# A gated MLP's first products with tokens on partitions, turned back through VectorE and DRAM

## The chip, the cores and the metric

The kernel runs on one core of one Trainium2 chip. The metric is the device time of one execution in microseconds. Five engines work side by side, each through its own list of instructions in order: TensorE (PE, with its weight loads PEld), VectorE (DVE), ScalarE (ACT), GpSimd (POOL) and SyncE (SP), which here only issues DMAs. An instruction whose input is late holds up everything behind it on its engine.

## The reference

One decoder layer on 256 tokens of width 2048, all in float32. The change is in its second half, the gated MLP:

```
h = rmsnorm(x, norm_ffn_w)                        # 256 x 2048
gate, up = split(h @ w_up, 2)                     # w_up 2048 x 11264, so 2 x (256 x 5632)
gate = causal_dwconv(gate, conv_ffn_w) + bias     # along the tokens, width 3, per feature
x = x + (gelu(gate) * up) @ w_down                # w_down 5632 x 2048
```

## The kernel before

Every float32 matrix is split into a rounded part and its remainder, `hi` and `lo` (type float32r), and a product is three: hi x hi, lo x hi, hi x lo.

**Weights.** `weights()` hands out the next tile of a fixed list `srcs`: 256 rows by 512 columns, 512 KB. `begin()` (L105 to L120) issues its load on SP into `raw` (four buffers, L110), ACT rounds it into `whi` (three buffers, L112), and DVE subtracts to get `wlo` (three buffers, L119). It does so two tiles ahead. The order in which each engine runs its instructions is not the order of the code: a scheduler of the framework arranges the rows of each engine at build time by its own idea of the times, and the order is then fixed.

**Two forms of product.** `gemm_a` (L138) keeps tokens on the partitions of the result: the activations are the stationary side (128 x 128) and the weights move, 512 columns at a time. For each of 16 slices of 128 rows and each of the two token halves it issues three matmuls of 512 columns (L149, L150, L151), 96 for a product of 2048 by 512. It first runs what stands in the list `later` after its first weight tile. `gemm_b` (L157) keeps features on partitions: the weights are stationary, and the activations' `hi` and `lo`, side by side in `fhl` (256 tokens each), move. For each slice and each of four groups of 128 features it issues one matmul of 512 columns (whi with hi and lo, L173) and one of 256 (wlo with hi, L174), 128 for a product. Its result has two halves for each group; `merged` (L178) copies one half out on ACT (L182) and adds the other on DVE (L183).

**The stage around the change** (L808 to L837) walks over the 5632 features in 11 blocks of 512. For a block: a `gemm_b` for gate; its merging; a multiplication by `rb2`, the norm's factor of each token laid along the free dimension (L814); the convolution along the tokens, 12 DVE instructions (L818, L822), which needs features on partitions; gelu on ACT (L824); a multiplication by `rb2` on POOL (L825); a `gemm_b` for up; its merging; the product with the gelu (L827); and the split of the result into `hhi` and `hlo` (L834, L835). These are the stationary side of the down stage (L854 to L864), 22 x 4 weight tiles of 12 matmuls each. Ahead of the stage stands the output projection, by `gemm_a` (L780 to L801).

**Block turns and DRAM elsewhere.** In the token mixer, four times, the kernel also writes a small tile to DRAM in pieces of 128 bytes (`cdd`, L554: 128 partitions of eight pieces), reads it back in another arrangement (`lb`, L557), and turns 32 x 32 blocks on DVE (L587, L621).

Of the kernel before, what the change touches and what calls it, by code (L numbers as in the profile page):

```python
# [33 lines left out]
def kernel(  # L34
# [32 lines left out]
    def nm(s):  # L67
        cnt[0] += 1
        return f"{s}_{cnt[0]}"

    def pg(shape=(P, 512)):
        return psg.tile(list(shape), F32, tag="g", name=nm("psg"))
# [26 lines left out]
    def weights():  # L99

        begin(taken[0] + AHEAD + 1)
        taken[0] += 1
        return made[taken[0] - 1]
# [28 lines left out]
    def pm():  # L132
        return psm.tile([P, 2, 512], F32, tag="m", name=nm("psm"))


    later = []

    def gemm_a(lh, ll, nk, steps=None, ps=None):  # L138

        ps = pm() if ps is None else ps  # L140
        for c in range(nk // 2) if steps is None else steps:
            if c == 1:
                while later:
                    later.pop(0)()
            hi, lo = weights()
            for kk in range(2):
                k = 2 * c + kk
                for t in range(2):
                    mm(ps[:, t, :], lh(k, t), hi[:, kk, :], start=(k == 0), stop=False)  # L149
                    mm(ps[:, t, :], ll(k, t), hi[:, kk, :], start=False, stop=False)  # L150
                    mm(ps[:, t, :], lh(k, t), lo[:, kk, :], start=False, stop=(k == nk - 1))  # L151
                side()
        return ps

    banks = [0]

    def gemm_b(rhl, nk):  # L157

        banks[0] ^= 1
        if banks[0]:
            pair = [pm(), pm()]
            ps = [pair[f // 2][:, f % 2].rearrange("p (a s) -> p a s", a=2) for f in range(4)]
        else:
            ps = [pg([P, 2, S]) for f in range(4)]
        for c in range(nk // 2):
            hi, lo = weights()
            for f in range(4):
                fs = slice(f * P, (f + 1) * P)  # L170
                for kk in range(2):
                    k = 2 * c + kk
                    mm(ps[f], hi[:, kk, fs], rhl(k), start=(k == 0), stop=False, skip_group_check=True)  # L173
                    mm(ps[f][:, 1, :], lo[:, kk, fs], rhl(k)[:, 0, :], start=False, stop=(k == nk - 1),  # L174
                       skip_group_check=True)
        return ps

    def merged(ps, dst):  # L178

        for f in range(4):  # L180
            low_half = fp.tile([P, S], F32, tag="lh", bufs=3, name=nm("lh"))
            nc.scalar.copy(low_half, ps[f][:, 1, :])  # L182
            nc.vector.tensor_tensor(dst[:, f, :], ps[f][:, 0, :], low_half, op=ALU.add)  # L183
        return dst

    def turned(src):

# [11 lines left out]
    ones = cpool.tile([P, P], F32, name="ones")  # L199
    nc.gpsimd.memset(ones, 1.0)  # L200
    ident = cpool.tile([P, P], F32, name="ident")
# [27 lines left out]
    for k2 in range(KD // 2):  # L229
        pt = pg([P, 2, S])  # L230
        for kk in range(2):
            k = 2 * k2 + kk
# [3 lines left out]
        for kk in range(2):  # L236
            k = 2 * k2 + kk
            nc.scalar.activation(xhi[:, k, :], pt[:, kk, :], AF.Copy, scale=nmw[:, k : k + 1])  # L238
            nc.vector.scalar_tensor_tensor(xlo[:, k, :], pt[:, kk, :], nmw[:, k : k + 1], xhi[:, k, :].bitcast(F32),
                                           op0=ALU.mult, op1=ALU.subtract)  # L240
# [47 lines left out]
    gwb = mp.tile([P, P], F32, name="gwb")  # L288
    nc.scalar.dma_start(gwb, gdn_norm_w[0].partition_broadcast(P))

    def rstd_rows(ssq, dst):


        ms = cpool.tile([P, 2], F32, name=nm("ms"))
        nc.vector.tensor_scalar(ms, ssq, 1.0 / D, EPS, op0=ALU.mult, op1=ALU.add)
        rs = cpool.tile([P, 2], F32, name=nm("rs"))
        nc.gpsimd.tensor_tensor(rs, ms, epsx, op=ALU.pow)
        if dst is None:
            return rs
        pr = pg()  # L300
        for t in range(2):
            dg = cpool.tile([P, P], F32, tag="diag", bufs=2, name=nm("diag"))
            nc.vector.tensor_scalar(dg, ident, rs[:, t : t + 1], None, op0=ALU.mult)
            mm(pr[:, t * P : (t + 1) * P], ones, dg, start=True, stop=True)
        nc.vector.tensor_copy(dst, pr[:, :S])
        return rs

    ssq4 = cpool.tile([P, 2, 4], F32, tag="ssq4", name="ssq4a")
# [3 lines left out]
            nc.scalar.activation(junk, x0[c][:, t, :], AF.Square, accum_out=ssq4[:, t, c : c + 1])  # L312
    ssq = cpool.tile([P, 2], F32, name="ssq")
    nc.vector.tensor_reduce(ssq, ssq4, axis=mybir.AxisListType.X, op=ALU.add)
    rs1 = rstd_rows(ssq, None)
    rsh = cpool.tile([P, 2], F32, name="rsh")
    nc.vector.tensor_scalar(rsh, rs1, 0.5, None, op0=ALU.mult)
    rsq = cpool.tile([P, 2], F32, name="rsq")
# [27 lines left out]
    for cq in range(4):  # L346
        pr = slice(32 * cq, 32 * cq + 32)
# [18 lines left out]
    for c in range(2):  # L366
        hi, lo = weights()
        for kk in range(8):
            k = 8 * c + kk
# [57 lines left out]
    for g, win in enumerate(WINDOWS):  # L427
# [3 lines left out]
        for cs in (slice(0, P + PAD), slice(P + PAD, NB)):  # L431
            b = bd[:, cs]
# [255 lines left out]
    for g in range(4):  # L688
        kq = mp.tile([P, 4, 2, S], F32, tag="kq", bufs=1, name=nm("kq"))
        vT = mp.tile([P, 4, S], F32, tag="vT", bufs=1, name=nm("vT"))  # L690
        for kind, dst in ((1, kq[:, :, 0, :]), (0, kq[:, :, 1, :]), (2, vT)):
# [3 lines left out]
            ps = ps_k0 if kind == 1 and g == 0 else gemm_a(xh, xl, KD)  # L695
            e = evict(ps)
# [5 lines left out]
        ps = gemm_a(xh, xl, KD)  # L702
        e = evict(ps)
# [97 lines left out]
                                               op0=ALU.mult, op1=ALU.subtract)  # L801
    ssq2 = cpool.tile([P, 2], F32, name="ssq2")
    nc.vector.tensor_reduce(ssq2, ssq4, axis=mybir.AxisListType.X, op=ALU.add)
    rb2 = cpool.tile([P, S], F32, tag="rb", name="rb2")
    rstd_rows(ssq2, rb2)


    hhi = []  # L808
    hlo = []
    rb2b = rb2.unsqueeze(1).to_broadcast([P, 4, S])  # L810
    for c in range(DFF // 512):
        ps = gemm_b(lambda k: fhl[:, k], KD)
        gs = fp.tile([P, 4, S], F32, tag="gs", bufs=2, name=nm("gs"))
        nc.vector.tensor_tensor(gs, merged(ps, gs), rb2b, op=ALU.mult)  # L814
        y = fp.tile([P, 4, S], F32, tag="y", name=nm("y"))
        for f in range(4):
            r = 4 * c + f
            nc.vector.tensor_scalar(y[:, f, :], gs[:, f, :], cfw[:, 2 * KF + r : 2 * KF + r + 1],  # L818
                                    vec[:, V_CB + r : V_CB + r + 1], op0=ALU.mult, op1=ALU.add)
            for j in (1, 0):  # L820
                s = 2 - j
                nc.vector.scalar_tensor_tensor(y[:, f, s:], gs[:, f, : S - s], cfw[:, j * KF + r : j * KF + r + 1],  # L822
                                               y[:, f, s:], op0=ALU.mult, op1=ALU.add)
        nc.scalar.activation(y, y, AF.Gelu)  # L824
        nc.gpsimd.tensor_tensor(y, y, rb2b, op=ALU.mult)  # L825
        ps = gemm_b(lambda k: fhl[:, k], KD)
        nc.vector.tensor_tensor(gs, merged(ps, gs), y, op=ALU.mult)  # L827
        if c < 4:
            hh = mtile(c, [P, 4, S], F32R, f"hhi{c}")
            hl = mtile(4 + c, [P, 4, S], F32R, f"hlo{c}")  # L830
        else:
            hh = fp.tile([P, 4, S], F32R, name=f"hhi{c}")
            hl = fp.tile([P, 4, S], F32R, name=f"hlo{c}")
        nc.scalar.copy(hh, gs)  # L834
        nc.vector.tensor_tensor(hl, gs, hh.bitcast(F32), op=ALU.subtract)  # L835
        hhi.append(hh)
        hlo.append(hl)  # L837

    nfin = big.tile([P, D], F32, tag="xhl", name="nfin")
    nc.scalar.dma_start(nfin, norm_final_w.partition_broadcast(P))  # L840
# [75 lines left out]
```

## Time and profile before

| | |
|---|---|
| median of 3 runs | 1590.08 us (1589.59 to 1591.71) |
| span of the profiled execution | 1591.1 us |
| first matmul of gate and up to first of the down stage | 848.3 to 1341 us |
| down stage | 1341 to 1580 us |
| HBM read, written | 287.07 MB, 3.15 MB |

The profiled execution is one of its own; its span lies 1.0 us above the median. In a group's row stand line, engine, operation, output and inputs with shapes, count, then busy time in total, the mean of one in ns, and the engine's idle time just before them. Matmuls overlap in the pipeline, so the mean of one (390 ns) is longer than their spacing; the spacing is read from a stretch of time and the count in it.

### The profile page before, as it was taken

The page shows a single profiled execution, that of the slowest core. Times are in us where ns is not written, and L with a number is a line of the kernel's source. Part 1 is how long each engine was busy: PE and PEld are TensorE (multiplying, and loading weights), DVE is VectorE, ACT ScalarE, POOL GpSimd, SP SyncE. Part 2 cuts the span into 40 slices and gives each one's busy share as a digit, 9 for nine tenths or more (in the row PEclk, how much of TensorE's full clock was granted, in tenths as well). Part 3 has the DMA queues.
Part 4 walks back from the last instruction along what each step waited for, and adds up shares of the span by engine and source line. Part 5 has one row for each costly group of instructions (what it writes and reads, how often), then busy time and mean ns, then how long its engine had stood idle before and what let it go on. Part 6 is the DMA issues. An engine that isn't in the chain of part 4 may idle for free.

```text
span 1591.1 us, 21437 instructions
## 1 busy us (share of the span) xinstructions
PE 1568.4 (99%) x8116; PEld 1318.2 (83%) x8116; DVE 1065.8 (67%) x1624; ACT 750.2 (47%) x969; POOL 116.7 (7%) x132
## 2 busy tenths in 40 slices
PE   8999999999999999999999999999999999999997
PEld 6888888888888888787888888888888888888886
DVE  5778757786678757786565777666666677444445
ACT  5545435444545445544454544444444444333334
POOL 3020100110020100102000000000000000000000
PEclk9999999999999999999999999999999999999998
DMA  7656656566556656565656666666666666666563
GB/s 248 181 156 193 192 147 173 166 194 173 159 151 194 191 153 174 164 190 173 203 185 182 187 189 191 188 186 187 186 196 186 187 191 208 200 193 198 190 194 133
DMA packets 160605, 291.62 MB, mean 183 GB/s; under 512 B 18022, under 2 KB 21110, under 8 KB 160374
## 3 DMA queue, kind: packets, MB, share of 16 engines
q1 hardware_dynamic: 157792, 285.77, 61.2%
q10 hardware_dynamic: 2710, 4.48, 0.8%
q8 instruction: 63, 1.03, 0.3%
q14 instruction: 40, 0.33, 0.1%
HBM read 287.07 MB, written 3.15 MB: 182 GB/s over the span
## 4 chain that ended last, share of the span: by engine, by line
PE 89%; DMA 3%; DVE 3%; issue 2%; POOL 2%; SPq 1%; ACT 0%; DVEq 0%; POOLq 0%
PE psm L151 13%; PE psm L150 12%; PE psm L149 12%; PE psm L173 10%; PE psg L173 10%; PE psg L174 5%; PE psm L174 5%; PE psg L850 3%; PE psg L851 3%; PE psg L852 3%; PE psm L851 2%; PE psm L850 2%; PE psm L852 2%; DVE wlo L119 1%; PE psg L519 1%
## 5 line engine op out<-in xcount | busy, mean ns | idle before, releaser
L119 DVE TENSOR_TENSOR wlo<-raw,whi 128x1024 fp32r<-128x1024 f32 x528 | 657.2, 1246 | 412.9 <-ACT whi L112 406.6
L112 ACT CAST whi<-raw 128x1024 fp32r<-128x1024 f32 x530 | 557.8, 1053 | 752.7 <-PE psm L150 342.9
L151 PE MATMUL psm<-wlo,xhl 128*128 128x512 f32 x896 | 353.3, 394 | 2.9 <-DVE wlo L119 2.9
L149 PE MATMUL psm<-whi,xhl 128*128 128x512 f32 x896 | 352.5, 393 | 1.7 <-ACT xhl L238 1.7
L150 PE MATMUL psm<-whi,xhl 128*128 128x512 f32 x896 | 352.1, 393 | 0.0
L173 PE MATMUL psm<-fhl,whi 128*128 128x512 f32 x704 | 245.9, 396 | 0.0
L173 PE MATMUL psg<-fhl,whi 128*128 128x512 f32 x704 | 237.8, 394 | 0.0
L151 PEld LDWEIGHTS psm<-wlo,xhl 128*128 128x128 f32 x896 | 168.7, 188 | 38.7 <-DVE wlo L119 4.5
L149 PEld LDWEIGHTS psm<-whi,xhl 128*128 128x128 f32 x896 | 168.9, 188 | 35.7 <-ACT xhl L238 2.1
L150 PEld LDWEIGHTS psm<-whi,xhl 128*128 128x128 f32 x896 | 168.9, 188 | 34.9
L174 PE MATMUL psm<-fhl,wlo 128*128 128x256 f32 x704 | 194.2, 279 | 0.0
L174 PE MATMUL psg<-fhl,wlo 128*128 128x256 f32 x704 | 178.6, 279 | 0.0
L173 PEld LDWEIGHTS psm<-fhl,whi 128*128 128x128 f32 x704 | 131.3, 188 | 30.4
L173 PEld LDWEIGHTS psg<-fhl,whi 128*128 128x128 f32 x704 | 129.2, 188 | 24.1
L174 PEld LDWEIGHTS psg<-fhl,wlo 128*128 128x128 f32 x704 | 132.4, 188 | 6.9
L174 PEld LDWEIGHTS psm<-fhl,wlo 128*128 128x128 f32 x704 | 132.5, 188 | 1.1
L850 PE MATMUL psg<-whi,hhi 128*128 128x512 f32 x176 | 68.6, 390 | 0.0
L851 PE MATMUL psg<-whi,hlo 128*128 128x512 f32 x176 | 68.5, 389 | 0.0
L850 PE MATMUL psm<-whi,hhi 128*128 128x512 f32 x176 | 68.5, 389 | 0.0
L851 PE MATMUL psm<-whi,hlo 128*128 128x512 f32 x176 | 68.5, 389 | 0.0
L852 PE MATMUL psm<-wlo,hhi 128*128 128x512 f32 x176 | 68.5, 389 | 0.0
L852 PE MATMUL psg<-wlo,hhi 128*128 128x512 f32 x176 | 61.6, 389 | 0.0
(233 smaller groups left out, 1515.7 us busy)
## 6 DMA issues: line engine op xcount, KB each, us to landing
raw<-in_w_in_dram SPq DMA_DIRECT2D x226, 512.0 KB, 3.8
raw<-in_w_up_dram SPq DMA_DIRECT2D x176, 512.0 KB, 3.8
raw<-in_w_down_dram SPq DMA_DIRECT2D x88, 512.0 KB, 3.7
raw<-in_w_out_dram SPq DMA_DIRECT2D x32, 512.0 KB, 3.7
raw<-in_pool_w_dram SPq DMA_DIRECT2D x8, 512.0 KB, 3.9
x<-in_x_dram SPq DMA_DIRECT2D x4, 512.0 KB, 7.7
lb<-cdd SPq DMA_DIRECT2D x16, 128.0 KB, 2.9
xt<-in_x_dram ACTq DMA_DIRECT2D x4, 512.0 KB, 7.9
```

The lines of the kernel that those rows point to most:

```text
L112: nc.scalar.copy(hi, raw)
L119: nc.vector.tensor_tensor(lo, raw, hi.bitcast(F32), op=ALU.subtract)
L149: mm(ps[:, t, :], lh(k, t), hi[:, kk, :], start=(k == 0), stop=False)
L150: mm(ps[:, t, :], ll(k, t), hi[:, kk, :], start=False, stop=False)
L151: mm(ps[:, t, :], lh(k, t), lo[:, kk, :], start=False, stop=(k == nk - 1))
L173: mm(ps[f], hi[:, kk, fs], rhl(k), start=(k == 0), stop=False, skip_group_check=True)
L174: mm(ps[f][:, 1, :], lo[:, kk, fs], rhl(k)[:, 0, :], start=False, stop=(k == nk - 1), skip_group_check=True)
L519: mm(pg0, kq[:, h, 0, 0:P], kq[:, h, :, :], start=True, stop=True)
L850: mm(acc[c][t], lh(k, t), hi[:, kk, :], start=(k == 0), stop=False)
L851: mm(acc[c][t], ll(k, t), hi[:, kk, :], start=False, stop=False)
L852: mm(acc[c][t], lh(k, t), lo[:, kk, :], start=False, stop=(k == KF - 1))
```

## The change

Gate and up are computed by `gemm_a`, tokens on partitions, 96 matmuls of 512 columns each; `gemm_b`, `merged` and `rb2` go. `features` evicts the result on ACT with the token's norm factor as scale (L788 of the new program), two instructions of 512 columns. `flip` then moves features to partitions: DVE turns every 32 x 32 block of the 128 x 1024 tile in one instruction (L158), four DMAs (L162), one for each 32 partitions, write the blocks to a DRAM tile of 512 features by 256 tokens in pieces of 32 tokens (128 bytes, 1024 pieces a DMA), and one DMA (L164) reads that tile back with features on partitions, in pieces of 1 KB. All five are issued on SP. The convolution and gelu, and the product and split, become functions that are put on `later`, and so are written into the code after the first weight tile of the next product. `y` and the gate's result have two buffers each. The other functions are as they were.

```
+    def flip(pool, src, tag, bufs):
+        b = pool.tile([P, 2, 512], F32, tag="tn", name=nm("tn"))
+        nc.vector.transpose(b.rearrange("p t f -> p (t f)"), src.rearrange("p t f -> p (t f)"))
+        d = dpool.tile([512, S], F32, tag="flip", name=nm("flip"))
+        dv = d.rearrange("(f i) (t a j) -> a i t f j", i=32, t=2, j=32)
+        for a in range(4):
+            nc.sync.dma_start(dv[a], b[32 * a : 32 * a + 32].rearrange("p t (f j) -> p t f j", j=32))
+        o = pool.tile([P, 4, S], F32, tag=tag, bufs=bufs, name=nm(tag))
+        nc.sync.dma_start(o, d.rearrange("(f p) s -> p f s", p=P))
+        return o
...
+    rs2 = rstd(ssq2)
...
+    def features(ps):
+        e = fp.tile([P, 2, 512], F32, tag="ev", name=nm("fev"))
+        for t in range(2):
+            nc.scalar.activation(e[:, t, :], ps[:, t, :], AF.Copy, scale=rs2[:, t : t + 1])
+        return flip(fp, e, "gs", 2)
...
-    rb2b = rb2.unsqueeze(1).to_broadcast([P, 4, S])
-    for c in range(DFF // 512):
-        ps = gemm_b(lambda k: fhl[:, k], KD)
-        gs = fp.tile([P, 4, S], F32, tag="gs", bufs=2, name=nm("gs"))
-        nc.vector.tensor_tensor(gs, merged(ps, gs), rb2b, op=ALU.mult)
-        y = fp.tile([P, 4, S], F32, tag="y", name=nm("y"))
+    def gated_linear(c, gs, y):
         for f in range(4):
...
         nc.scalar.activation(y, y, AF.Gelu)
-        nc.gpsimd.tensor_tensor(y, y, rb2b, op=ALU.mult)
-        ps = gemm_b(lambda k: fhl[:, k], KD)
-        nc.vector.tensor_tensor(gs, merged(ps, gs), y, op=ALU.mult)
+
+    def product(us, y, hh, hl):
+        nc.vector.tensor_tensor(y, us, y, op=ALU.mult)
+        nc.scalar.copy(hh, y)
+        nc.vector.tensor_tensor(hl, y, hh.bitcast(F32), op=ALU.subtract)
+
+    for c in range(DFF // 512):
+        gs = features(gemm_a(fh, fl, KD))
+        y = fp.tile([P, 4, S], F32, tag="y", bufs=2, name=nm("y"))
+        later.append(lambda c=c, gs=gs, y=y: gated_linear(c, gs, y))
+        us = features(gemm_a(fh, fl, KD))
...
+        later.append(lambda us=us, y=y, hh=hh, hl=hl: product(us, y, hh, hl))
...
+    while later:
+        later.pop(0)()
```

The scheduler's order in the stage, at the two places of which the prediction speaks. Weight tiles of `w_up` are numbered from 0, eight to a product, so the gate product of the second block has tiles 16 to 23; names carry running numbers.

SP, after that gate product. Before, its rows in the whole stage are weight loads alone, one like the other. Now (raw_7916 is tile 30, raw_7934 tile 31, raw_7952 tile 32, raw_7970 tile 33):

```order
L110 DMA raw_7898<-in_w_up_dram 128x2x512
L110 DMA raw_7916<-in_w_up_dram 128x2x512
L162 DMA flip_7822<-tn_7820 64x16x32 x4
L110 DMA raw_7934<-in_w_up_dram 128x2x512
L110 DMA raw_7952<-in_w_up_dram 128x2x512
L164 DMA gs_7827<-flip_7822 128x4x256
L110 DMA raw_7970<-in_w_up_dram 128x2x512
```

The four writes stand behind the load of tile 30; the loads of tiles 31 and 32 come between the writes and the read, and four more loads after tile 33's follow before the next product's writes.

DVE, from a gate product's end to the end of the next product. Before (the gate product ends ahead of the first L183 row; `psm` is its result, `lh` the copied half):

```order
L183 TENSOR_TENSOR gs_8334<-psm_8156,lh_8335 128x256
L119 TENSOR_TENSOR wlo_8371<-raw_8367,whi_8369 128x1024
L183 TENSOR_TENSOR gs_8334<-psm_8156,lh_8338 128x256
L183 TENSOR_TENSOR gs_8334<-psm_8157,lh_8341 128x256
L119 TENSOR_TENSOR wlo_8393<-raw_8389,whi_8391 128x1024
L183 TENSOR_TENSOR gs_8334<-psm_8157,lh_8344 128x256
L814 TENSOR_TENSOR gs_8334<-gs_8334,rb_7335 128x1024
L119 TENSOR_TENSOR wlo_8415<-raw_8411,whi_8413 128x1024
L818 TENSOR_SCALAR y_8348<-gs_8334,cfw,vec 128x256 x4
L822 SCALAR_TENSOR_TENSOR y_8348<-gs_8334,cfw,y_8348 128x255 x3
```

Now (wlo_7835 is tile 26, the third after the gate product's end; wlo_7920 is tile 30, wlo_7938 tile 31, wlo_7956 tile 32; `fev` is the evicted result, `tn` the turned one, `gs` what the read brings):

```order
L119 TENSOR_TENSOR wlo_7835<-raw_7831,whi_7833 128x1024
L158 STREAM_TRANSPOSE tn_7820<-fev_7817 128x1024
L119 TENSOR_TENSOR wlo_7866<-raw_7862,whi_7864 128x1024
L119 TENSOR_TENSOR wlo_7884<-raw_7880,whi_7882 128x1024
L119 TENSOR_TENSOR wlo_7902<-raw_7898,whi_7900 128x1024
L119 TENSOR_TENSOR wlo_7920<-raw_7916,whi_7918 128x1024
L797 TENSOR_SCALAR y_7829<-gs_7827,cfw,vec 128x256 x4
L801 SCALAR_TENSOR_TENSOR y_7829<-gs_7827,cfw,y_7829 128x255 x4
L119 TENSOR_TENSOR wlo_7938<-raw_7934,whi_7936 128x1024
L801 SCALAR_TENSOR_TENSOR y_7829<-gs_7827,cfw,y_7829 128x254 x4
L119 TENSOR_TENSOR wlo_7956<-raw_7952,whi_7954 128x1024
```

Before, the convolution stood two weight tiles behind the end of its product and read what DVE itself had just written; now it stands four tiles behind the turn and reads what a DMA brings. After an up product, the product with the gelu (L806) has the convolution's place, with one wlo behind it, then the split.

More of the change, by code (lines that the diff above doesn't have):

```diff
@@ L153, in gemm_a @@
         return ps
[L155 to L184, printed above, removed]
+    def flip(pool, src, tag, bufs):
[8 more added lines that the diff above has]
+        return o
     def turned(src):
@@ L289, with rstd @@
     nc.scalar.dma_start(gwb, gdn_norm_w[0].partition_broadcast(P))
-    def rstd_rows(ssq, dst):
+    def rstd(ssq):
         ms = cpool.tile([P, 2], F32, name=nm("ms"))
@@ L297, in rstd_rows @@
         nc.gpsimd.tensor_tensor(rs, ms, epsx, op=ALU.pow)
[L298 to L305, printed above, removed]
         return rs
@@ L314 @@
     nc.vector.tensor_reduce(ssq, ssq4, axis=mybir.AxisListType.X, op=ALU.add)
-    rs1 = rstd_rows(ssq, None)
+    rs1 = rstd(ssq)
     rsh = cpool.tile([P, 2], F32, name="rsh")
@@ L803, with fh, fl @@
     nc.vector.tensor_reduce(ssq2, ssq4, axis=mybir.AxisListType.X, op=ALU.add)
-    rb2 = cpool.tile([P, S], F32, tag="rb", name="rb2")
-    rstd_rows(ssq2, rb2)
+    rs2 = rstd(ssq2)
+    def fh(k, t):
+        return fhi[:, k, t * P : (t + 1) * P]
+    def fl(k, t):
+        return flo[:, k, t * P : (t + 1) * P]
+    def features(ps):
[3 more added lines that the diff above has]
+        return flip(fp, e, "gs", 2)
     hhi = []
     hlo = []
-    rb2b = rb2.unsqueeze(1).to_broadcast([P, 4, S])
-    for c in range(DFF // 512):
-        ps = gemm_b(lambda k: fhl[:, k], KD)
-        gs = fp.tile([P, 4, S], F32, tag="gs", bufs=2, name=nm("gs"))
-        nc.vector.tensor_tensor(gs, merged(ps, gs), rb2b, op=ALU.mult)
-        y = fp.tile([P, 4, S], F32, tag="y", name=nm("y"))
+    def gated_linear(c, gs, y):
         for f in range(4):
@@ L833 @@
             hl = fp.tile([P, 4, S], F32R, name=f"hlo{c}")
-        nc.scalar.copy(hh, gs)
-        nc.vector.tensor_tensor(hl, gs, hh.bitcast(F32), op=ALU.subtract)
+        later.append(lambda us=us, y=y, hh=hh, hl=hl: product(us, y, hh, hl))
         hhi.append(hh)
         hlo.append(hl)
+    while later:
+        later.pop(0)()
     nfin = big.tile([P, D], F32, tag="xhl", name="nfin")
```

## The prediction

> **What bounds the kernel now.** I read the engine totals, then the chain that ended last, then the groups of instructions, then a table by stretches of time.
>
> ```profile
> PE 1568.4 (99%) x8116; PEld 1318.2 (83%) x8116; DVE 1065.8 (67%) x1624; ACT 750.2 (47%) x969; POOL 116.7 (7%) x132
> PE 89%; DMA 3%; DVE 3%; issue 2%; POOL 2%; SPq 1%; ACT 0%; DVEq 0%; POOLq 0%
> L173 PE MATMUL psm<-fhl,whi 128*128 128x512 f32 x704 | 245.9, 396 | 0.0
> L174 PE MATMUL psm<-fhl,wlo 128*128 128x256 f32 x704 | 194.2, 279 | 0.0
> ```
> ```profile
> 1360.00:1560.00 200.00, 200.00 (x884) 165.59 (x883) 89.50 (x74) 78.07 (x74) 0.00 (x0) 1.00 0.62 194
> 848.30:1341.00 492.70, 492.70 (x2828) 430.21 (x2827) 336.84 (x434) 238.72 (x293) 28.05 (x12) 1.00 0.64 188
> ```
>
> TensorE is busy 99% of the span and makes up 89% of the chain; the matmuls of gate and up waited 0.0 us. The second fence holds, for each stretch, its length and the busy time (and count) of PE, PEld, DVE, ACT and POOL, then the granted clock, the DMA share and GB/s. In 848.30 to 1341.00, the stretch of gate and up, PE never stops, so the time there is the number of matmuls times their spacing. Nothing that DVE, ACT or POOL does there costs anything, unless it makes PE wait.
>
> **PE, the gain.** Of 2828 matmuls, 2816 are the 1408 pairs of a 512 wide and a 256 wide one; the other 12 are small and take about 1.2 us (eight 128 wide ones ran 1.05 us, row in the fence below). So a product of 64 pairs takes (492.7 - 1.2) / 22 = 22.34 us. The new form has 96 matmuls, all 512 wide, the form of the down stage, where the first row gives 200.00 / 884 = 0.2262 us each: 21.72 us. The columns streamed are equal (64 x 768 = 96 x 512), so the 0.62 us are what the narrow matmuls cost beyond their width. 22 x 0.62 = **13.7 us** gained if PE still never waits.
>
> **DVE, ACT, POOL, off the path.**
>
> ```profile
> 757.02 1.05 PE L648 MATMUL psg<-w,ga 128*128 128x128 f32 x8
> L183 DVE TENSOR_TENSOR gs<-psm,lh 128x256 f32<-128x256 f32 x44 | 17.4, 417 | 0.0
> L814 DVE TENSOR_TENSOR gs<-gs,rb 128x1024 f32<-128x1024 f32 x11 | 13.5, 1225 | 0.4
> L182 ACT COPY lh<-psg 128x256 f32<-128x256 f32 x44 | 16.3, 370 | 4.3 <-PE psg L174 2.0
> L450 ACT ACTIVATE ev<-psm,rs 128x512 f32<-128x512 f32 x32 | 20.2, 681 | 1.6 <-PE psm L151 1.6
> L587 DVE STREAM_TRANSPOSE tcm<-tct x4: 445/446/448, 179.4 to 718.8; 128x256 f32<-128x256 f32 x4
> L621 DVE STREAM_TRANSPOSE TT<-T 32x128 f32<-32x128 f32 x16 | 4.8, 302 | 0.5
> ```
>
> DVE loses 88 additions of 0.417 and 11 scalings of 1.225 us (50 us) and gains 22 turns of 1024 columns. No row has that size: 256 columns took 446 ns and 128 took 302, 1.125 ns a column, so about 1.3 us (four times 446, 1.8, at most): 29 to 39 us. ACT loses 88 copies of 0.37 and gains 44 evictions of 0.68 us: even. POOL loses the scaling of L825. All that is covered by PE. On SP come 110 more DMAs: per product four writes and one read.
>
> **The new chain, and where it can reach PE.** Count from t = 0, the end of a gate product, in the order shown on DVE (tile 24 is then the next on PE). The tempo of the other engines:
>
> ```profile
> 762.21 1.05 ACT L112 CAST whi<-raw 128x1024 fp32r<-128x1024 f32 x1 [1.67 <-PE psm L150]
> 762.24 0.39 PE L149 MATMUL psm<-whi,mhi 128*128 128x512 f32 x1
> 763.30 1.23 DVE L119 TENSOR_TENSOR wlo<-raw,whi 128x1024 fp32r<-128x1024 f32 x1 [1.50 <-ACT whi L112]
> ```
> ```profile
> 661.01 0.40 SPq L554 DMA_DIRECT2D cdd<-cd  x1
> 665.68 1.90 SPq L557 DMA_DIRECT2D lb<-cdd  x4
> raw<-in_w_up_dram SPq DMA_DIRECT2D x176, 512.0 KB, 3.8
> ```
>
> A cast starts as PE ends a tile (three buffers), the subtraction follows, done 2.3 us after the tile's end. So: cast to 1.05, eviction 2 x 0.68 to 2.4, turn 1.3, hand-overs 0.1: the block is turned at **3.9**. Then the writes. The one in the trace of this kind is cdd: 1024 pieces of 128 bytes, as one of the four here. Its packets by stretch (1.00 us of the burst, its fastest quarter, and a stretch of another such write with weights between, 0.50 us; then a weight load, 2 KB packets, 1.25 us, and by stretches its fastest 0.5 us):
>
> ```profile
> DMA packets 1043, 0.22 MB, mean 224 GB/s; under 512 B 997, under 2 KB 997, under 8 KB 1042
> DMA packets 358, 0.05 MB, mean 213 GB/s; under 512 B 357, under 2 KB 357, under 8 KB 357
> q1 hardware_dynamic: 357, 0.04, 115.4%
> DMA packets 473, 0.14 MB, mean 276 GB/s; under 512 B 432, under 2 KB 432, under 8 KB 473
> q1 hardware_dynamic: 473, 0.14, 124.7%
> DMA packets 207, 0.41 MB, mean 329 GB/s; under 512 B 6, under 2 KB 6, under 8 KB 207
> q1 hardware_dynamic: 207, 0.41, 91.6%
> ...
> 904.50:905.00 0.50, 0.50 (x4) 0.43 (x4) 0.50 (x1) 0.00 (x0) 0.00 (x0) 1.00 1.00 389
> ```
>
> That is 864 to 1428 pieces a microsecond; I take 1000, the mean of a whole burst. 4096 pieces need 4.1 us (2.9 to 4.7). The loads show some 1.75 us from issue to the bulk of the packets and 0.6 from the last packet to landing (3.8 less 1.4 to 1.5 of data; estimates). Written: 3.9 + 1.75 + 4.1 = 9.75; SP issues the read at 10.4. But two weight loads stand ahead of it in SP's order, behind the writes: 0.524 MB at 389 GB/s, 1.35 us each, to 12.45. The read, 512 KB in pieces of 1 KB, 1.6 us (by the two rates, 389 and 329 GB/s, 1.35 to 1.6; smaller packets, so the slower), and landing: **14.6**, with bounds 13.4 and 15.2 from the piece rate.
>
> Who waits: the convolution on DVE for that read; behind it stands the subtraction of tile 31, and PE for that. PE starts tile 31 at 7 x 2.715 = 19.0 and reads its wlo 0.45 later; tile 32's at 22.2. DVE needs, after the read lands,
>
> ```profile
> L818 DVE TENSOR_SCALAR y<-gs,cfw,vec 128x256 f32<-128x256 f32 x44 | 15.2, 408 | 0.0
> L822 DVE SCALAR_TENSOR_TENSOR y<-gs,cfw,y 128x255 f32<-128x255 f32 x44 | 19.2, 479 | 0.0
> L119 DVE TENSOR_TENSOR wlo<-raw,whi 128x1024 fp32r<-128x1024 f32 x528 | 657.2, 1246 | 412.9 <-ACT whi L112 406.6
> ```
>
> 4 x 0.408 + 4 x 0.479 = 3.55, wlo 1.24, 4 x 0.478 = 1.9, wlo 1.24: 7.9 us, to 22.2. So a gate block may land as late as **14.3**; each microsecond later is one of PE, 11 times. An up block only has a 1.23 us product and one wlo before 19.5: limit 17.0. The six weight loads queued behind the read on SP are due at 10.5 and need 3.8 us before their cast at 19.0: 4.7 us of cover. The last blocks of the stage have the whole down stage; its accumulator that waits for the last eviction (2.5) comes fourth in turn (8.1).
>
> The sum: 1591.1 (the profiled span) - 13.7 + 11 x 0.3 (14.6 against 14.3) = 1580.7; the median of the runs is 1.0 below that span, so **1580**. With 13.4 it is 1576, with 15.2 (0.9 late) 1586: the forecast's own range, with 2 us for the rate of PE, is 1574 to 1588.
>
> The Trainium skill ("DMA: Bandwidth & Descriptors", "Rules for kernel authors") warns against a plain DMA with a rearranged pattern for a transposition, 19 times slower than the hardware's. By it a block would take 19 x 1.35 = 26 us, an estimate, longer than a product, and the sum would be some 1912 us. The rows disagree: 128-byte pieces cost 2.9 to 4.7 us a block, two to four times a weight load, since the turn of 32 x 32 blocks on DVE leaves them whole.
>
> **Rivals.** (a) *The block lands late.* The four writes take from 32 partitions each, cdd from 128, and four follow one another; no row shows either. At two thirds of my rate (665 a us) they take 6.2 us, the block lands at 16.7, 2.4 late: 1576 + 26, **1602**; at half, 18.7: gates 4.4, ups 1.7 late, 11 x 6.1 = 67, about 1643. It turns slower from 15.8 on (11 x 1.5 = 13.7 + 3). For it: one hand-over of 1 us that I missed suffices. Against: the trace's writes at full pace. (b) *The DMA engines fill.* By time of packets: 0.64 x 22.4 = 14.3 us a product now; 16 x 0.25 x 1.154 / 357 = 13 ns a piece (21 by the slower stretch), 4096 / 16 of them 3.3 to 5.4; the read at 88 ns, 2.8: 20.4 to 22.5 of 21.7. For it, that sum; against, that packet times stretch when nobody waits: 0.41 MB in 1.25 us is 329 GB/s, and 5.2 MB in 21.7 only 241. If it holds, loads queue and a product takes some 24 us: 1591 + 22 x 1.7 = 1628. (c) *The crossing paces the stage.* At 200 pieces a microsecond, a fifth of the row, the writes take 20.5 us; with 8 x 1.35 of weights and 1.6 of read the queue needs 33 us a product: 1591 + 22 x 10.5 = 1822. For it: scattered 1 KB steps in DRAM; against: cdd scatters as widely. The Trainium skill's rule above would act here as this does. (d) *No gain*: the wide matmuls run at 0.233 here, or the lateness eats the gain: 1590. Against the first: the same form at 0.2262 in the down stage, with as much DMA.
>
> **How the numbers follow.** Forecast 0.55; (a) 0.22; (b) 0.06; (c) 0.02; (d) 0.15, mostly lateness between 15.3 and 15.8. This kernel's measurement tells no less than 0.2%, 3 us, from no change, so faster 0.55, same 0.15, slower 0.30. The time is that of the forecast. The range goes from 1574 to 1620 (landing 17.6: 3.3 and 0.6 late, 1576 + 43), leaving 0.03 below and 0.12 above, for half the rate, (c) and part of (b).
>
> **What would show it.** Matmul spacing 0.226 in the stage, and a stage of 478 to 482 us instead of 492.7. The first convolution (L797) waits for a DMA, and the wlo behind it is what PE waits for, in the last tile before or the first of the next gate product, 0 to 1 us each. The turn near 1.3 us, and 128-byte packets near 1000 a us. If PE waits elsewhere, for casts or raw tiles, then (b); if it waits over 1.5 us at each gate, then (a). I am wrong if the stage is longer than 492 us, or if PE is gapless with pairs no cheaper.

## The result, and the profile after

The changed kernel takes 1581.36 us (1580.43 to 1587.84), the kernel before, beside it, 1589.80 (1589.55 to 1591.71): a ratio of **0.9949, with a 95% interval of 0.9935 to 0.9964**. The prediction was 1580, in a range of 1574 to 1620. The profiled execution of the changed kernel took 1581.35 us, its span is 1579.6.

The engine totals and the shares of the chain that ended last, of the changed kernel:

```profile
PE 1556.7 (99%) x7408; PEld 1284.3 (81%) x7408; DVE 1040.2 (66%) x1544; ACT 745.8 (47%) x925; POOL 89.4 (6%) x121
PE 86%; DMA 4%; DVE 4%; issue 3%; SPq 1%; POOL 1%; ACT 0%; DVEq 0%; POOLq 0%
```

PE is busy 11.7 us less than the 1568.4 of before and still makes up 86% of the chain. Next, stretches of the stage (length, busy time and count of PE, PEld, DVE, ACT and POOL, granted clock, DMA share, GB/s). First the kernel before:

```profile
860.00:1330.00 470.00, 470.00 (x2695) 410.24 (x2694) 320.69 (x411) 225.10 (x274) 24.86 (x10) 1.00 0.65 189
```

Then the changed kernel, whose last row is the down stage:

```profile
860.00:1330.00 470.00, 468.12 (x2058) 385.34 (x2057) 300.00 (x343) 224.81 (x235) 0.00 (x0) 1.00 0.79 237
1360.00:1560.00 200.00, 200.00 (x884) 165.62 (x883) 90.40 (x74) 77.47 (x74) 0.00 (x0) 1.00 0.57 190
```

PE now has short gaps in the stage. Summed over the starts of successive matmuls, by how much each start came later than 0.2262 us after the last (differences under 0.01 us left out), they are 3.8 us; (470 - 3.8) / 2058 is 0.2265 us, so between the gaps the wide matmuls run at the down stage's pace. The DMA share rose from 0.65 to 0.79.

The waits of the stage (us in total, times, longest) show what makes the gaps:

```profile
DVE y L806 <- DMA gs<-flip: 30.9, 10, 3.6
DVE y L797 <- DMA gs<-flip: 23.1, 11, 3.7
PEld psm L151 <- DVE wlo L119: 4.8, 7, 1.4
PE psm L151 <- DVE wlo L119: 1.4, 2, 0.9
```

DVE waits at each of the 11 convolutions (L797) and at 10 of the products (L806) for the block read back; of that, PE sees a few microseconds, through a late `wlo`. One gate block in order of time (start, length, engine, line; the gate product ends at 999.38, the prediction's t = 0):

```profile
999.38 1.05 ACT L112 CAST whi<-raw 128x1024 fp32r<-128x1024 f32 x1 [1.62 <-PE psm L150]
1000.34 1.26 ACT L788 ACTIVATE fev<-psm,rs 128x512 f32<-128x512 f32 x2
1001.63 1.25 DVE L158 STREAM_TRANSPOSE tn<-fev 128x1024 f32<-128x1024 f32 x1
1002.90 4.42 SPq L162 DMA_DIRECT2D flip<-tn  x4
1007.42 1.15 SPq L110 DMA_DIRECT2D raw<-in_w_up_dram  x2
1009.87 0.37 SPq L164 DMA_DIRECT2D gs<-flip  x1
1015.07 1.38 DVE L797 TENSOR_SCALAR y<-gs,cfw,vec 128x256 f32<-128x256 f32 x4 [2.50 <-DMA gs<-flip]
1017.95 1.21 DVE L119 TENSOR_TENSOR wlo<-raw,whi 128x1024 fp32r<-128x1024 f32 x1
1020.66 3.48 DVE L119 TENSOR_TENSOR wlo<-raw,whi 128x1024 fp32r<-128x1024 f32 x3
```

The block is turned at 3.5, its read issued at 10.5, and it has landed at 15.7. It is one of 11: the convolutions of the gate blocks start 13.9 to 16.9 us after their product's end, 15.3 on average. The latest, where the gate product ends at 1086.9, and PE at its first gap:

```profile
1103.79 1.38 DVE L797 TENSOR_SCALAR y<-gs,cfw,vec 128x256 f32<-128x256 f32 x4 [3.73 <-DMA gs<-flip]
1107.94 0.50 PE L151 MATMUL psm<-wlo,fhl 128*128 128x512 f32 x1 [0.94 <-DVE wlo L119]
```

The turn and the issues of the writes (ns, shortest, median and longest):

```profile
L162 SPq DMA_DIRECT2D flip<-tn x88: 581/667/3589, 872.1 to 1340.0; - x88
L158 DVE STREAM_TRANSPOSE tn<-fev x22: 1230/1245/1247, 870.8 to 1332.9; 128x1024 f32<-128x1024 f32 x22
```

And the DMA issues (KB each, median us from issue to landing):

```profile
raw<-in_w_up_dram SPq DMA_DIRECT2D x176, 512.0 KB, 4.5
flip<-tn SPq DMA_DIRECT2D x88, 128.0 KB, 4.7
gs<-flip SPq DMA_DIRECT2D x22, 512.0 KB, 4.7
```

**A measure for the experiments.** The work ahead of the stage is the same code in most of these kernels, yet its end moves by a few microseconds between profiled executions (the stage's first matmul stood at 848.3 us before, at 845.9 in the changed kernel, at 851.2 in another run). Where a trace is spoken of below, I therefore count from that first matmul to the end of the span: before 1591.1 - 848.3 = 742.8 us, now 1579.6 - 845.9 = 733.7, 9.1 us less.

### The profile page after: what moved, and what is told of

Its sections match the earlier page's. It is cut to its first block, busy times and chain, and to the rows that moved or that the text cites. A ratio compares the mean times of both kernels' runs of the same rounds, so it can differ in the third digit from the quotient of the medians.

```text
span 1579.6 us, 20017 instructions
## 1 busy us (share of the span) xinstructions
PE 1556.7 (99%) x7408; PEld 1284.3 (81%) x7408; DVE 1040.2 (66%) x1544; ACT 745.8 (47%) x925; POOL 89.4 (6%) x121
## 4 chain that ended last, share of the span: by engine, by line
PE 86%; DMA 4%; DVE 4%; issue 3%; SPq 1%; POOL 1%; ACT 0%; DVEq 0%; POOLq 0%
PE psm L151 22%; PE psm L150 21%; PE psm L149 21%; PE psg L840 3%; PE psm L839 3%; PE psg L839 2%; PE psm L838 2%; PE psg L838 2%; PE psm L840 2%; DVE wlo L119 2%; DMA gs<-flip 1%; SPq L162 1%; PE psg L491 1%; DMA flip<-tn 1%; PE psg L175 1%
## 5 line engine op out<-in xcount | busy, mean ns | idle before, releaser
L119 DVE TENSOR_TENSOR wlo<-raw,whi 128x1024 fp32r<-128x1024 f32 x528 | 648.5, 1233 | 376.1 <-ACT whi L112 368.6
L151 PE MATMUL psm<-wlo,fhl 128*128 128x512 f32 x704 | 273.7, 390 | 1.9 <-DVE wlo L119 1.4
L150 PE MATMUL psm<-whi,fhl 128*128 128x512 f32 x704 | 274.0, 389 | 0.0
L149 PE MATMUL psm<-whi,fhl 128*128 128x512 f32 x704 | 273.9, 389 | 0.0
L151 PEld LDWEIGHTS psm<-wlo,fhl 128*128 128x128 f32 x704 | 132.1, 188 | 32.0 <-DVE wlo L119 4.8
L150 PEld LDWEIGHTS psm<-whi,fhl 128*128 128x128 f32 x704 | 132.2, 188 | 27.6
L149 PEld LDWEIGHTS psm<-whi,fhl 128*128 128x128 f32 x704 | 132.2, 188 | 27.1
L439 DVE SCALAR_TENSOR_TENSOR cy<-psg,cqw,cy 128x255 f32<-128x255 f32 (+1 forms) x144 | 60.5, 473 | 0.4 <-ACT cy L436 0.4
L151 PE MATMUL psm<-wlo,mhi 128*128 128x512 f32 x128 | 50.0, 391 | 0.3 <-DVE wlo L119 0.3
```

What stands on the lines that cost most here:

```text
L119: nc.vector.tensor_tensor(lo, raw, hi.bitcast(F32), op=ALU.subtract)
L439: nc.vector.scalar_tensor_tensor(y[:, f, s:], gs[:, : S - s], w(j), y[:, f, s:], op0=ALU.mult, op1=ALU.add)
```

## Experiments

The theory: the pace of the wide matmuls gives 13.7 us, and the wait of the convolution for the block read back takes some 4 of them. The rivals for the missing part are that the pace is worth less, that the added traffic costs, or that one of the queues does. All diffs are against the changed kernel. The times of before, beside the runs, were 1591.9 to 1592.05 us.

### 1. Without the way through DRAM

The turn writes straight into the tile that the convolution reads; the features then lie in the wrong places.

```
-        b = pool.tile([P, 2, 512], F32, tag="tn", name=nm("tn"))
-        nc.vector.transpose(b.rearrange("p t f -> p (t f)"), src.rearrange("p t f -> p (t f)"))
...
-        for a in range(4):
-            nc.sync.dma_start(dv[a], b[32 * a : 32 * a + 32].rearrange("p t (f j) -> p t f j", j=32))
...
-        nc.sync.dma_start(o, d.rearrange("(f p) s -> p f s", p=P))
+        nc.vector.transpose(o.rearrange("p f s -> p (f s)"), src.rearrange("p t f -> p (t f)"))
```

> Leaves out the way through DRAM: the 32x32 block turn on VectorE writes straight into the tile that the convolution and the product read, so features stand in the wrong places, but every other instruction is there. Theory (the pace of the wide matmuls is worth 13.7 us and the PE gaps of 3.8 us in the changed kernel come from blocks that land late): no gaps are left, the stage runs at 0.2262 us a matmul, 1577.5 us (1576.5 to 1578.5), 4 us under the changed kernel. Rival (the crossing is hidden, and what is missing of the gain is the pace itself): 1581, as the changed kernel.

Measured: 1578.80 us, ratio 0.9915 [0.9903, 0.9927]; from the stage's start to the end 729.6 us, 13.2 less than before. The same stretch of the stage:

```profile
860.00:1330.00 470.00, 470.00 (x2075) 389.20 (x2074) 306.19 (x347) 229.20 (x239) 0.00 (x0) 1.00 0.66 193
```

No gap is left on PE. So the pace is worth 13.2 us of the 13.7 predicted, and the way through DRAM costs 733.7 - 729.6 = 4.1, against 3.8 us of gaps. This says that the way through DRAM costs it, not yet how.

### 2. The convolution held two weight tiles later

The way through DRAM and its traffic stay whole. The convolution is put into the order of DVE behind the subtraction of tile 32, and the product with the gelu comes two tiles later as well. (`subs` lists the subtractions; `issue_after` places what it encloses behind one of them.)

```
     def gated_linear(c, gs, y):
+        with tc.issue_after(subs[taken[0] - 1].ins):
+            convolved(c, gs, y)
...
     def product(us, y, hh, hl):
-        nc.vector.tensor_tensor(y, us, y, op=ALU.mult)
+        with tc.issue_after(subs[taken[0] - 1].ins):
+            nc.vector.tensor_tensor(y, us, y, op=ALU.mult)
...
+        if c:
+            later.append(prod)
+        us = features(gemm_a(fh, fl, KD))
         later.append(lambda c=c, gs=gs, y=y: gated_linear(c, gs, y))
-        us = features(gemm_a(fh, fl, KD))
...
-        later.append(lambda us=us, y=y, hh=hh, hl=hl: product(us, y, hh, hl))
+        prod = lambda us=us, y=y, hh=hh, hl=hl: product(us, y, hh, hl)
```

> The change whole, and on VectorE the convolution is queued two weight tiles later (behind the subtraction of tile 32 of the prediction's count, done near 18.6 us after the gate product's end, while the block lands near 15.7), the product with the gelu two tiles later too. Theory (only the order on VectorE makes PE wait for a block): no gaps of PE in the stage, as without the way through DRAM, so 0.9915 of the kernel before, 1576.5 to 1579. Rival (the blocks' DMAs slow the weights themselves, or a later convolution makes the next turn late and the wait moves there): gaps remain, 1581 or more.

Measured: 1579.18 us, ratio 0.9919 [0.9905, 0.9933]; 730.1 us from the stage's start. The stage, and DVE around one convolution (its line is L805 here, the subtraction's L120):

```profile
860.00:1330.00 470.00, 470.00 (x2076) 389.16 (x2075) 305.11 (x347) 228.45 (x239) 0.00 (x0) 1.00 0.83 240
```
```profile
1017.11 1.22 DVE L120 TENSOR_TENSOR wlo<-raw,whi 128x1024 fp32r<-128x1024 f32 x1 [1.50 <-ACT whi L113]
1018.25 1.38 DVE L805 TENSOR_SCALAR y<-gs,cfw,vec 128x256 f32<-128x256 f32 x4
```

The convolution starts without a wait, and PE has no gap, at a DMA share of 0.83, higher than the changed kernel's 0.79. So the traffic itself costs nothing; all of the 4 us comes from the place in DVE's order of what reads the block: it stood ahead of a `wlo`, and waited there.

To be sure of so small a difference, both ran again side by side on one chip:

> The whole change with the convolution held behind the subtraction of tile 32, again, on the same chip as the changed kernel as it is. Theory (its gain is the 3.8 us of PE gaps that the wait for the read back costs): ratio 0.992, about 3 us below the changed kernel beside it. Rival (the difference between the two was one of chips): the two agree within 1 us.

> The changed kernel as it is, beside the one with the convolution held later. Theory: ratio 0.9945 to 0.995, PE gaps of 3 to 5 us at the gates. Rival: 0.992, no different from the held one.

Measured: held later 1580.16 us, 0.9923 [0.9911, 0.9935], 729.7 us from the stage's start; as it is 1584.58 us, 0.9954 [0.9942, 0.9967], 733.8, with 3.5 us of PE gaps. The difference is 4.4 us. Not all of these gaps stand at the gates: 1.2 us of them lie behind three up blocks, where it is the product with the gelu (L806) that waits. For one of them, whose up product ends at 1022.3:

```profile
1040.41 1.22 DVE L806 TENSOR_TENSOR y<-gs,y 128x1024 f32<-128x1024 f32 x1 [4.45 <-DMA gs<-flip]
1042.83 0.50 PE L151 MATMUL psm<-wlo,fhl 128*128 128x512 f32 x1 [0.38 <-DVE wlo L119]
```

So holding the product later is part of the remedy too. Holding both later beats both kernels.

### 3. The read back on another queue

```
-        nc.sync.dma_start(o, d.rearrange("(f p) s -> p f s", p=P))
+        nc.gpsimd.dma_start(o, d.rearrange("(f p) s -> p f s", p=P))
```

> Only the read back of the block is issued on GpSimd's queue in place of SP's, so it no longer stands behind two weight loads. Theory (lateness decides, and about 2.7 us of it is those two loads): the block lands 2 to 2.7 us earlier, near 13.3 us after the product's end where the limit is some 15, the gaps before the first tiles of a gate product vanish: 1577.5 to 1578.5. Rival (the two loads are not what delays it, or GpSimd's queue is slower to start by as much): 1581 or more.

Measured: 1603.29 us, ratio 1.0075 [1.0062, 1.0089]. The prediction's chain has the read behind two weight loads in SP's order; I expected it to land earlier if it had a queue of its own. It landed later:

```profile
gs<-flip POOLq DMA_DIRECT2D x22, 512.0 KB, 5.9
```
```profile
DVE y L797 <- DMA gs<-flip: 38.5, 10, 4.3
PEld psm L151 <- DVE wlo L119: 25.7, 28, 1.9
```
```profile
1025.92 1.38 DVE L797 TENSOR_SCALAR y<-gs,cfw,vec 128x256 f32<-128x256 f32 x4 [4.06 <-DMA gs<-flip]
```

From issue to landing took 5.9 us instead of 4.7. The start makes the difference, as the rival has it: on GpSimd's queue the read's first packet comes 2.8 to 4.1 us after the issue, on SP's 1.6 to 2.4, while the packets then take about as long (2.4 us on average, 2.6 on SP's queue) among about as many bytes of weights (0.40 MB, 0.36). In the block of the last row the gate product ends at 1008.67 and the convolution starts 17.2 us later; over the 11 gate blocks it is 17.1 us on average, in the changed kernel 15.3. The convolutions waited 38.5 us instead of 23.1, and PE's gaps came to 23 us instead of 3.8. So 1.8 us more lateness multiplied the price of the crossing by six, as the prediction's rival (a) has it ("It turns slower from 15.8 on").

The two loads ahead of the read, which I took for a cost that could be avoided, did not hold up its issue. In the changed kernel SP issues them while the writes are under way, and what it then waits for, here over the whole stage, is the landing of the writes:

```profile
SPq L164 <- DMA flip<-tn: 24.8, 32, 1.3
```

A queue of the read's own has that wait as well.

### 4. Writes and read on that queue

The same edit for the four writes too.

> The four writes and the read are issued on GpSimd's queue. Theory (SP's queue held by the writes is what delays, 4.4 us of issue a block): SP's weight loads flow as before, the blocks land by 14, 1577.5 to 1579. Rival (making 1024 descriptors a DMA takes GpSimd longer than SP): the writes take several us more, the block lands after 16, gaps of 1 to 5 us at each gate, 1590 to 1630.

Measured: 1592.48 us (1585.76 to 1600.18 in ten executions), ratio 1.0004 [0.9988, 1.0020], no different from before. Writes and reads both take 5.6 us to land:

```profile
flip<-tn POOLq DMA_DIRECT2D x88, 128.0 KB, 5.6
gs<-flip POOLq DMA_DIRECT2D x22, 512.0 KB, 5.6
```

The rival held: the gate blocks come 16.6 to 21.5 us after their product's end, not by 14. PE's gaps in the profiled execution are 14.7 us (1.5 of them matmuls at half the granted clock, behind a gap of 3.3 us), and 744.8 us pass from the stage's start, 2.0 more than before: 13.2 gained and 14.7 lost are 1.5. The queue is not all that changed: five `wlo` now stand between a turn and its convolution on DVE and six between a turn and its product, where the changed kernel has four. That order moves the limit to some 18 us (a gate block at 17.6 left no gap, one at 18.3 cost 0.3 us) and so spares PE much of the wait; this run does not price the queue alone. The spread of these executions is wider than any other kernel's here; what makes it so was not settled.

### 5. Each block written twice

Four more writes for each block, to a DRAM tile that nothing reads.

```
+        d2 = dpool.tile([512, S], F32, tag="flip2", name=nm("flip2"))
+        dv2 = d2.rearrange("(f i) (t a j) -> a i t f j", i=32, t=2, j=32)
+        for dd in (dv2, dv):
+            for a in range(4):
+                nc.sync.dma_start(dd[a], b[32 * a : 32 * a + 32].rearrange("p t (f j) -> p t f j", j=32))
```

> Each block is written to DRAM twice, first to a tile that nobody reads: four more writes of 1024 pieces stand ahead of the read. Theory (each microsecond of a block beyond its limit is one of PE): the block lands some 4.5 us later, near 20 us; 4.5 to 5 us at each gate and 2 to 3 at each up block, 11 times: 70 to 90 us on 1579, so 1650 to 1670, more if the clock falls in gaps that long. Rival (the crossing has room, the gaps of the changed kernel are chance): under 1600.

Measured: 1610.72 us (two executions, 1606.83 and 1614.60), ratio 1.0117 [1.0089, 1.0145]. The size was missed, by some 50 us: I had taken the order on DVE as it was, and the scheduler put the convolution one `wlo` later and the product two, so that the convolution's wait for the block stayed as it was. Instead weight loads came late:

```profile
DVE wlo L119 <- ACT whi L112: 163.7, 82, 6.8
ACT whi L112 <- DMA raw<-in_w_up_dram: 122.3, 55, 7.0
...
DVE y L800 <- DMA gs<-flip: 23.0, 10, 3.4
```
```profile
860.00:1330.00 470.00, 454.75 (x1971) 368.66 (x1970) 284.45 (x324) 214.68 (x225) 0.00 (x0) 1.00 0.90 250
```
```profile
1009.60 7.04 SPq L165 DMA_DIRECT2D flip<-tn  x8
1016.74 1.68 SPq L110 DMA_DIRECT2D raw<-in_w_up_dram  x3
```

The casts (`whi`) waited 122.3 us for weights. The third fence is SP's own time: eight writes occupy it for 7.0 us, and the loads behind them are issued only then. The DMA share is 0.90 on average and GB/s hardly rose (250 after 237). Whether SP's issue or the fill of the DMA engines makes the loads late, this run can't tell apart; it shows how near rival (b) stood: with twice the pieces its sign came, casts that wait for weights, and the kernel took 15.8 us more than before (1604.7 - 846.1 = 758.6 from the stage's start) where the rival was priced at 37.

### 6. Turning on TensorE instead

The old way of this kernel, `turned`, takes the place of the turn on DVE and of the way through DRAM.

```
-        return flip(fp, e, "gs", 2)
+        return e
...
-    def gated_linear(c, gs, y):
+    def gated_linear(c, e, y):
+        pts = turned(e)
...
+        for f2, pt in enumerate(turned(us)):
+            fs = slice(2 * f2, 2 * f2 + 2)
+            nc.vector.tensor_tensor(y[:, fs, :], pt, y[:, fs, :], op=ALU.mult)
```

> The evicted result is turned by TensorE (eight 128 by 128 transposes a product, as elsewhere in the kernel) in place of the block turn and the way through DRAM. Theory (PE is the bound, each transpose costs it about 0.11 us, the spacing of other 128 wide ones): 22 x 8 x 0.11 = 19 us on 1577.5, so 1597, slower than the kernel before. Rival (the transposes fit in gaps or are cheap): 1580.

Measured: 1599.85 us, ratio 1.0052 [1.0038, 1.0067]; 750.5 us from the stage's start, 20.9 more than without any crossing. That is 22 x 8 = 176 transpositions on PE at 0.119 us. PE has no gaps, it has more to do. The way through DRAM, at 4.1 us in the changed kernel and none when held later, is the cheaper one because it takes nothing from PE.

### 7. The change for gate alone, and for up alone

The other half of the products stays with `gemm_b`, `merged` and `rb2`. For gate alone:

```
-        us = features(gemm_a(fh, fl, KD))
+        while later:
+            later.pop(0)()
+        nc.gpsimd.tensor_tensor(y, y, rb2b, op=ALU.mult)
+        us = fp.tile([P, 4, S], F32, tag="gs", bufs=2, name=nm("us"))
+        merged(gemm_b(lambda k: fhl[:, k], KD), us)
```

> Only gate in the new form; up as before, with features on partitions. Theory: half of the pace, 6.9 us gained, less the gate blocks' gaps (3.8 us in the changed kernel): 0.9970 to 0.9985 of the kernel before, some 1586. Rival (the gain is not the pace of the matmuls, so it doesn't halve): as the whole change or none.

> Only up in the new form; gate as before. Theory: half of the pace, 6.9 us gained, and no gaps, since behind an up block's wait stands a single product of 1.23 us (limit 17 us): 0.9957 of the kernel before, some 1583. Rival as for gate only; if up blocks land late too, 1586.

Measured: gate alone 1629.05 us, ratio 1.0232 [1.0217, 1.0247]; up alone 1613.08 us, 1.0133 [1.0119, 1.0147]. Both missed by far. `gemm_b` takes the two wide accumulators (`psm`) for every other product, and `gemm_a` of the next product then has to wait until `merged` has emptied one. For gate alone, and then for up alone:

```profile
PE psm L149 <- DVE us L195: 23.5, 5, 4.8
```
```profile
PE psm L149 <- DVE gb L195: 16.2, 6, 2.7
```

In the changed kernel all products take one accumulator of two, and in the kernel before they alternate between `psm` and `psg`, so neither waits. The mixture was my own edit's fault; it says nothing on the halves. Gaps of this length cost more than themselves: the last section has the rows. Mended, with `gemm_b` in the one-bank accumulators alone (this diff is against the first versions):

```
-        banks[0] ^= 1
-        if banks[0]:
-            pair = [pm(), pm()]
-            ps = [pair[f // 2][:, f % 2].rearrange("p (a s) -> p a s", a=2) for f in range(4)]
-        else:
-            ps = [pg([P, 2, S]) for f in range(4)]
+        ps = [pg([P, 2, S]) for f in range(4)]
```

> The new form for the gate products alone, the up products as before, but with their sums always in the four one-bank accumulators (psg), so that no gate product has to wait for the two wide accumulators (psm), which is what the run with alternating accumulators showed (PE waiting for L195, 23.5 us). Theory (11 of 22 products at the cheaper pace, 11 x 0.6 = 6.9 us, less at most the 3.8 us that the convolution's wait costs at the gates in the changed kernel, and no clock loss): 6.9 to 3.1 us less than before, ratio 0.9957 to 0.998. Rival (the halves of the change are worth nothing alone, because a wide product that follows a split one costs PE something at the seam whatever the accumulators): ratio 1.00 or above, with PE gaps at the seams.

> The new form for the up products alone, the gate products as before with their sums always in the one-bank accumulators. An up block has 17.0 us before the first subtraction that PE needs, so the crossing should cost nothing. Theory: 6.9 us less than before and no PE gaps, ratio 0.9957. Rival (seams cost, whatever the accumulators): 1.00 or above. That gate alone and up alone add up to the whole change (minus 9 us) is the check on both.

Measured: gate alone 1588.00 us, ratio 0.9970 [0.9959, 0.9982], as the theory has it; 739.3 us from the stage's start, 3.5 less than before. Up alone 1591.40 us, 0.9995 [0.9986, 1.0003], a miss: I expected 0.9957. From the stage's start it does take 736.4 us, 6.4 less than before, and PE is gapless there:

```profile
865.00:1330.00 465.00, 465.00 (x2369) 395.89 (x2369) 316.00 (x387) 224.60 (x255) 0.00 (x0) 1.00 0.73 215
```

But the stage starts at 853.65 instead of 848.3 us. The first gate product now needs one-bank accumulators too, and those it cannot have before the norm's small products have run:

```profile
849.98 1.09 PE L801 MATMUL psg<-ident,xt 128*128 128x128 f32 x8 [1.31 <-DVE xt L792]
853.40 0.60 PE L311 MATMUL psg<-diag,ones 128*128 128x128 f32 x2 [2.33 <-DVE diag L310]
853.65 0.77 PE L180 MATMUL psg<-fhl,whi 128*128 128x512 f32 x1
```
```profile
853.60:856.80 3.20, 3.20 (x12) 2.71 (x12) 0.24 (x1) 0.00 (x0) 0.00 (x0) 0.50 0.14 55
```

Before, that product had `psm`, and PE worked on it while DVE prepared the diagonals. It is the seam to the output projection that costs here, once, and not the seams between the two forms. Inside the stage the halves give 3.5 and 6.4 us, together 9.9 against the whole change's 9.1. Half the pace is 6.9 us by the prediction. Up keeps it, as an estimate: its count leaves out the twelve small matmuls that in the kernel before stand behind the stage's start (about 1.2 us), and holds 3.2 us at half the granted clock behind the waits of PE (0.50 in the last row, 1.6 us lost), so 6.4 - 1.2 + 1.6 = 6.8. Gate loses 3.4 us to gaps, 2.7 of them where the down stage begins, behind the last `gemm_b` and its merging, and 0.7 at the gates and in the stage's first microseconds.

## Why the prediction was right, and where it was right by luck

- **PE, the gain.** 13.7 us from 22 products predicted; 13.2 measured without the crossing (experiment 1), 12.7 and 13.1 when held later. The wide form runs at 0.2262 us here as in the down stage, and rival (d) in its first form ("the wide matmuls run at 0.233 here") falls.
- **DVE, ACT, POOL.** Off the path as said. The turn took 1.245 us, where 1.3 was taken from two smaller sizes.
- **The chain up to the read.** Turned at 3.5 (predicted 3.9), read issued at 10.5 (10.4). That agreement hides a step that the prediction does not have: SP needs 4.4 us to issue the four writes, 2.4 of them for the third. The last section has what the pieces do meanwhile. The Trainium skill's rule on plain DMAs with a rearranged pattern ("DMA: Bandwidth & Descriptors", "Rules for kernel authors", 19 times slower) does not hold for this one: four writes of 1024 pieces are through in at most 7 us from the first issue (1002.90 to 1009.87), not the 26 estimated by it, since the turn on DVE leaves the pieces at 128 bytes.
- **The landing, 14.6, is the term that was mis-sized**: 15.3 on average over the gate blocks, 13.9 to 16.9, and five of the 11 beyond its upper bound of 15.2. In the block shown the read took 5.2 us from issue to use (1009.87 to 1015.07), not 4.2: its packets are spread over 2.9 us (1.9 to 3.5 in the 22 reads), among those of weight loads, where I had let it run alone, 1.6 us, at a weight load's rate.
- **The limit, 14.3, was off by as much.** DVE needs 7.9 us from the landing to the end of tile 32's `wlo` by the sum of its rows; it took 6.8 (1015.07 to 1021.85, the first of the three subtractions in the last row of the block). Four instructions that the rows give as 4 x 0.408 are one row of 1.38: successive ones overlap. PE stood 0.4 us for that subtraction, so the limit lay near 15.3. The other gate blocks say the same. The six that came by 15.1 us left no gap; those at 15.5, 15.7, 16.4 and 16.9 us cost PE 0.3, 0.4, 1.1 and 1.6 us, close to what each lay beyond 15.3 (the eleventh, at 16.5 and with the down stage behind it, cost 0.4). So "each microsecond later is one of PE" is right, block by block.
- **The 3.8 us are near the forecast's 11 x 0.3 by luck.** I had every gate block late by the same 0.3 us. In truth the average block was just in time, and the blocks' spread, which the prediction does not have, makes the gaps: two blocks bring 2.7 of the 3.8 us. Two errors, 0.7 us in the landing and 1.0 in the limit, hid this. With the landing alone put right, the sum would have been 11 x 0.7 = 8 us higher, 1588; with the limit alone, 1577 and no gap.
- **Up blocks** cost nothing in the profiled execution, as predicted, but with far less room: they came 15.6 to 16.7 us after their product's end, against a limit of 17.0, where I had counted on a gate block's 14.6. In the second profiled execution (experiment 2) three came at 17.2 to 18.1 us and cost 1.2 us. The last block of the stage, at 17.7 us, cost nothing, as predicted.
- **Rivals.** (a) was the real danger, and experiment 3 is it: 1.8 us later on average, and the change loses. (b) was weighed rightly: with one write of each block the loads are in time for PE at a DMA share of 0.79 to 0.83; with two they aren't. (c) and the second form of (d) did not come about.

## What to carry to other kernels

Where TensorE never waits, count the matmuls by form from a stretch without gaps: narrower ones cost more per column, and the difference times their number is the gain, to half a microsecond here. What such a change adds elsewhere is free as long as nothing on an in-order engine waits ahead of what PE needs next; so place the consumer of a slow transfer behind the last instruction that PE needs in that time, not at the earliest point at which its data might be there. That placement was worth 4 of 13 us, and experiment 2 needed no further buffer for it. Count the room block by block, too: with lateness that varies, an average just in time still costs what the late blocks cost. A mixture of two forms has to be checked for accumulators first.

## What the runs showed that I had not expected

**A gap of PE is followed by slow matmuls.** Gate alone (the first version), behind a gap of 4.8 us that ends at 900.9; the third figure from the end is the granted clock:

```profile
901.00:904.00 3.00, 3.00 (x7) 2.34 (x8) 1.73 (x3) 1.07 (x2) 0.00 (x0) 0.50 0.83 277
904.00:907.00 3.00, 3.00 (x11) 2.40 (x10) 1.32 (x2) 1.40 (x2) 0.00 (x0) 0.75 0.08 29
```

For some 4.5 us the clock is half, and a gap of 4.8 us costs about 7. Up alone (the first version) has gaps of 2.75 us, after one of which the clock fell and after another not:

```profile
875.80:880.00 4.20, 4.20 (x20) 3.46 (x20) 3.99 (x9) 1.16 (x2) 0.00 (x0) 1.00 0.40 127
967.20:972.20 5.00, 5.00 (x13) 3.89 (x12) 4.93 (x11) 0.57 (x1) 0.00 (x0) 0.50 0.34 104
```

The Trainium skill ("TensorE: Matmul & The Clock Gate", "Part 1: The HAM clock gate") says that the array falls to half its clock after an idle window of about 3.4 us. The traces agree on the half; here a gap of 2.75 us was enough at times. The gaps of the changed kernel, 1.1 us at most, left the clock at 1.00.

**A write of many pieces holds up the queue that issues it.** Of the four issues of a block, three take about 0.65 us and the third 2.4 in the block shown (1.0 to 3.6 in the stage, the longest in the row of L162 above). That third issue, then packets of the changed kernel while it stands (from 1005.5 us), while the fourth is issued (1006.9) and after it (1007.4), 0.50 us each:

```profile
1004.24 2.37 SPq L162 DMA_DIRECT2D flip<-tn  x1
DMA packets 614, 0.12 MB, mean 239 GB/s; under 512 B 592, under 2 KB 592, under 8 KB 614
DMA packets 264, 0.03 MB, mean 67 GB/s; under 512 B 264, under 2 KB 264, under 8 KB 264
DMA packets 773, 0.10 MB, mean 197 GB/s; under 512 B 773, under 2 KB 773, under 8 KB 773
```

The pieces run at about 1200 a microsecond while SP is held by the third issue, sink to 500 while the fourth is issued, and reach 1500 behind it. So a rate of pieces from a whole burst, 1000 a microsecond, was right on average (4096 in some 4.4 us) and is no steady rate. Why the third issue waits, no run here tells.
